# Loading the modulation rows of a two-layer recurrent backbone through GpSimd's DMA queue instead of SyncE's

## Chip, cores and metric

One Trainium2 chip, one core. The metric is the device time of one execution in microseconds. A core has five engines that run their own instruction streams in order: TensorE (PE, matmul; PEld is its weight load), VectorE (DVE), ScalarE (ACT), GpSimd (POOL) and SyncE (SP). Transfers between DRAM and on-chip memory (SBUF) are issued by an engine's instruction stream as DMAs and done by 16 DMA engines; an instruction that has to wait for a semaphore holds up all that stand behind it on its engine.

## What is computed

```python
for layer in range(2):
    mod_l = silu(c) @ w_ada[layer] + b_ada[layer]         # 6 x 1024: shift, scale, gate, twice
    mod_c = silu(c_ctx) @ w_ada[layer] + b_ada[layer]
    pl = split_proj(modulate(xl, sh1_l, sc1_l) @ w_in[layer])      # xl: 1024 latent tokens x 1024
    pc = split_proj(modulate(xc, sh1_c, sc1_c) @ w_in[layer])      # xc: 256 context tokens
    mixed = hgrn2, mlstm, retention, gla of (pc, pl)               # forward and backward chunk scans
    xl = xl + g1_l * mixer_out(raw_l, pl, g_heads[layer], w_out[layer])
    xl = xl + g2_l * (relu(modulate(xl, sh2_l, sc2_l) @ w_ff1[layer]) ** 2 @ w_ff2[layer])
    # the context xc likewise, in layer 0 alone
return rmsnorm(xl) * g_final
```

All inputs are float32. The modulation vectors `mod` depend on the conditioning `c` and `c_ctx` alone: 2 layers x 6144 values x 2 conditionings, each a dot product over 1024.

## The kernel before

All 1280 tokens stay on the chip with the 1024 features in 8 tiles of 128 partitions. Dense products are done as three matmuls each, on values split into a high and a low part (`mm3`, L292 to L296). Weights come through `whalf` (L276): SP loads 128 x 512 floats into a small ring `st` (L281), ACT makes the high part (L282), DVE the low part (L283).

A layer has four stages: a norm with the modulation applied, the mixers (`mixers`, L1422), the output projection (`outproj`, L1508) and the MLP (`mlp`, L488). In `mixers` the scans of four head groups run on DVE, ACT and PE, and the dense projections that later groups need are mixed in as filler for PE (`Fill`, L157). Projections are written to DRAM from a ring of temporaries in `st` (L689, L734, L735, L743) and fetched again (L695, L756); outputs go out at L710, gates read them at L647 and store at L658; mLSTM loads its row factors at L1326.

The first third of layer 0's modulation is a matmul at the start. Its other two thirds and the three thirds of layer 1 are computed on DVE by `ada_rows` (L402) in slack time: for a third r, a conditioning j and a half h of the 1024 inputs, the conditioning is loaded broadcast to all partitions from the scratch tensor `d_c` (L410), then 16 tiles `w_adaR` of 128 rows x 512 inputs (256 KB each, L413), and each is multiplied by it and summed along the row by one DVE instruction (L414, shown in the profile as a SCALAR_TENSOR_TENSOR and a DVE_READ_ACCUMULATOR):

```python
c = cs.next()(512)
queue.dma_start(c..., self.d_c[j:j + 1, 4 * h:4 * h + 4, :].to_broadcast([128, 4, 128]))
for o in range(16):
    w = wring.next()(512)
    queue.dma_start(w, self.io["w_adaR"][l, r, o, :, 512 * h:512 * h + 512])
    nc.vector.scalar_tensor_tensor(w, w, 1.0, c, ..., accum_out=S[:, o:o + 1, h])
```

The function is called in two places, and `queue` is SP in both. In the mixers of layer 0 (`ada`, L1597) it makes 128 row loads into two buffers of the tile `ph`, with one conditioning buffer; `Fill.step` advances it at three of five filler steps. In the MLP of layer 0 (`ada1`, L1608, advanced by `filler`) it makes 128 row loads into five buffers (two in `pc`, three in `st`), again with one conditioning buffer. A row load waits until the L414 that last read its buffer is done.

POOL itself has little to do: the store of `d_c` at the start (L333), memsets of a column of ones for the mLSTM values (L768, ten in a layer), of two slices of the mLSTM state (L1291, L1292, two pairs in a layer), and five subtractions in the norm behind the MLP (L485). The order of the instructions on each engine comes from the framework's scheduler, which sees the dependences of the whole program.

Of the kernel before, what the change touches and what calls it, by code (L numbers as in the profile page):

```python
# [42 lines left out]
class Ring:  # L43
# [4 lines left out]
    def next(self):  # L48
        x = self.items[self.i % len(self.items)]
        self.i += 1  # L50
        return x
# [1521 lines left out]
def build(ctx, tc, io):  # L1573
    b = K(ctx, tc, io)
    b.setup()
    nc = b.nc
    b.l = 0
    b.openX()
    for k in range(NK):
        nc.scalar.dma_start(b.X[k][:, 0:CTX], io["xT"][:, k, 0:CTX])  # L1580
    b.params(b.tmps.next())

    ps, ss = b.pool("ps", [512] * 16)
    bk = b.banks.next()
    ring = Ring(ss)
    for k in range(NK):
        b.ada_unit(0, 0, k, bk, ring)
    b.ada_finish(0, 0, bk, b.banks.next(), b.tmps.next())
    ps.release()
    b.params2(b.tmps.next())  # L1590
    b.cond_rows(b.tmps.next())
    for l in range(2):
        b.l = l
        tbs = TBS if l == 0 else TBS[1:]
        b.mix_open(l)

        def ada(bufs):  # L1597
            for r in (1, 2):
                yield from b.ada_rows(0, r, (0, 1), Ring(bufs[:2]), Ring(bufs[2:]), nc.sync)
        b.mixers(l, ada)  # L1600
        b.outproj(l)
        na = 3
        nf = 2 if l == 0 else 0
        nw = (b.rest - NK * NT - na * 2 * NT - 512 * nf) // 1024
        pc, cs = b.pool(f"pc{l}", [1024] * nw + [512] * nf + [NT] * (2 * na))
        wring = Ring(cs[:nw])
        aring = Ring(zip(cs[nw + nf::2], cs[nw + nf + 1::2]))
        def ada1(bufs, l=l):  # L1608
            for r in range(3) if l == 0 else ():
                yield from b.ada_rows(1, r, (0, 1) if r == 0 else (1,), Ring(bufs[:5]), Ring(bufs[5:]), nc.sync, 2)  # L1610
        tmps = b.tmps
        gen = ada1(cs[nw:nw + nf] + tmps.items[4:])

        def filler():
            for _ in range(3):
                next(gen, None)
        if l == 0:
            b.tmps = Ring(tmps.items[:4])
        first = [b.wtile(io["w_ff1"][l, f], wring) for f in range(2)]
        b.norm_block(l, tbs[-1], 24, 32, fast=FAST[5])  # L1620

        def after(tb, l=l):
            if l == 1:
                b.final_block(tb)
            elif tb[0] != TBS[-1][0]:
                b.norm_block(1, tb, 0, 8, nc.gpsimd if tb[0] else None, FAST[6] if tb[0] else FAST[7])
        b.mlp(l, tbs, wring, aring, filler, first, after)
        b.tmps = tmps
        pc.release()
    b.final_norm(*b.late)  # L1630
    b.poolX.release()
# [110 lines left out]
```

## Time and profile before

| | us |
|---|---|
| median of 3 runs | 3276.86 (3276.39 to 3285.53) |
| the profiled execution | 3277.57, span 3275.8 |
| PE busy | 3188.0 (97%) |
| DVE busy | 2098.3 (64%) |
| ACT busy | 1285.0 (39%) |
| POOL busy | 11.5 |
| bytes read and written in HBM | 259.11 and 45.65 MB, 93 GB/s over the span |

Busy time leaves out instructions that only wait or issue a DMA; for POOL the issuing instruction is counted. An average over the span says little of a single stage: the stages have different limits, and what matters is which wait ends last in each. The span divides into the start (to about 40 us), layer 0's norm and mixers (to about 780), its output projection (to about 910), its MLP (to about 1800), and layer 1 in the same order. The changed loads lie between 226 and 720 us and between 915 and 1120 us.

### The profile page before, as it was taken

To read this page: it belongs to the slowest core of one execution; us is meant where nothing else is said; L and a number is where in the kernel's file an instruction comes from. 1 tells how busy PE (TensorE), PEld (TensorE's weight loads), DVE (VectorE), ACT (ScalarE), POOL (GpSimd) and SP (SyncE) were. 2 spreads that over 40 slices of the span, in tenths; PEclk is the share of its full clock that TensorE was granted. 3 is DMA by queue.
4 is the path that set the end of the run, shared out by engine and by line. 5 is a ranking of instruction groups with operands and counts; after the bars stand their busy time and mean duration, and the time that the engine had idled before them with its cause. 6 is when DMAs were issued, how large, how long until landed. Compare 5 with 4: busy or idle time off the path is not lost.

```text
span 3275.8 us, 52563 instructions
## 1 busy us (share of the span) xinstructions
PE 3188.0 (97%) x20681; PEld 2607.3 (80%) x20681; DVE 2098.3 (64%) x4333; ACT 1285.0 (39%) x2665; POOL 11.5 (0%) x42
## 2 busy tenths in 40 slices
PE   7999999999999999999999999999999999999998
PEld 4787788878888888888888677788778888888887
DVE  4778887776588845454545586876756555555546
ACT  4666564545332121212122575764444322222222
POOL 0000000000000000000000000000000000000000
PEclk9999899999999999999999999999999999999999
DMA  6115566345157511111111212333224111111111
GB/s 208 58 61 176 183 186 190 120 134 179 63 165 230 161 39 39 39 39 39 39 39 40 78 64 73 120 109 113 90 72 151 58 46 52 46 52 46 52 49 65
DMA packets 181953, 308.20 MB, mean 94 GB/s; under 512 B 21880, under 2 KB 51240, under 8 KB 181448
## 3 DMA queue, kind: packets, MB, share of 16 engines
q1 hardware_dynamic: 180376, 303.02, 28.8%
q8 instruction: 162, 2.65, 0.3%
q10 hardware_dynamic: 1296, 1.81, 0.2%
q14 instruction: 87, 0.71, 0.1%
q0 software_dynamic: 32, 0.01, 0.0%
HBM read 259.11 MB, written 45.65 MB: 93 GB/s over the span
## 4 chain that ended last, share of the span: by engine, by line
PE 81%; DVE 8%; DMA 6%; ACT 3%; issue 1%; SPq 0%; DVEq 0%; ACTq 0%
PE psum L294 22%; PE psum L295 21%; PE psum L296 21%; PE psum L831 2%; PE psum L601 2%; PE psum L834 1%; PE psum L818 1%; PE psum L632 1%; DMA ph<-w_adaR 1%; PE psum L634 1%; PE psum L633 1%; PE psum L1359 1%; PE psum L706 1%; PE psum L1019 1%; DMA ps<-w_ada 1%
## 5 line engine op out<-in xcount | busy, mean ns | idle before, releaser
L526 DVE SCALAR_TENSOR_TENSOR x<-psum,st,x 128x512 f32<-128x512 f32 (+1 forms) x648 | 440.7, 689 | 203.5 <-PE psum L296 202.8
L282 ACT ACTIVATE pc<-st 128x512 fp32r<-128x512 f32 x256 | 161.2, 632 | 854.4 <-PE psum L295 840.9
L295 PE MATMUL psum<-pc,pc 128*128 128x512 f32 (+1 forms) x1296 | 477.0, 368 | 6.0 <-DVE pc L506 6.0
L294 PE MATMUL psum<-pc,pc 128*128 128x512 f32 (+1 forms) x1296 | 476.1, 367 | 0.0
L296 PE MATMUL psum<-pc,pc 128*128 128x512 f32 (+1 forms) x1296 | 474.7, 366 | 0.0
L294 PE MATMUL psum<-Hhi,pc 128*128 128x512 f32 (+1 forms) x1280 | 471.1, 368 | 1.5 <-ACT pc L282 1.5
L295 PE MATMUL psum<-Hlo,pc 128*128 128x512 f32 (+1 forms) x1280 | 472.0, 369 | 0.1
L296 PE MATMUL psum<-Hhi,pc 128*128 128x512 f32 (+1 forms) x1280 | 470.5, 368 | 0.0
L294 PE MATMUL psum<-Hhi,pw 128*128 128x512 f32 (+1 forms) x1192 | 451.5, 379 | 7.6 <-ACT pw L282 3.5
L295 PE MATMUL psum<-Hlo,pw 128*128 128x512 f32 (+1 forms) x1192 | 447.5, 375 | 0.0
L296 PE MATMUL psum<-Hhi,pw 128*128 128x512 f32 (+1 forms) x1192 | 446.6, 375 | 0.6 <-DVE pw L283 0.6
L505 DVE TENSOR_TENSOR st<-st 128x256 f32<-128x256 f32 (+1 forms) x160 | 101.8, 637 | 301.5 <-ACT pc L504 300.8
L295 PEld LDWEIGHTS psum<-pc,pc 128*128 128x128 f32 x1296 | 245.0, 189 | 48.4 <-DVE pc L506 6.9
L294 PEld LDWEIGHTS psum<-pc,pc 128*128 128x128 f32 x1296 | 245.0, 189 | 44.1 <-DVE x L526 1.2
L296 PEld LDWEIGHTS psum<-pc,pc 128*128 128x128 f32 x1296 | 244.6, 189 | 42.9 <-issue 2.7
L294 PEld LDWEIGHTS psum<-Hhi,pc 128*128 128x128 f32 x1280 | 241.3, 189 | 43.3 <-ACT pc L282 2.4
L295 PEld LDWEIGHTS psum<-Hlo,pc 128*128 128x128 f32 x1280 | 241.3, 189 | 41.0 <-issue 0.5
L283 DVE TENSOR_TENSOR pc<-st,pc 128x512 fp32r<-128x512 f32 x256 | 175.6, 689 | 153.4 <-ACT pc L282 133.5
L296 PEld LDWEIGHTS psum<-Hhi,pc 128*128 128x128 f32 x1280 | 241.1, 188 | 41.0 <-DVE pc L283 0.6
L294 PEld LDWEIGHTS psum<-Hhi,pw 128*128 128x128 f32 x1192 | 227.3, 191 | 53.7 <-issue 9.2
L296 PEld LDWEIGHTS psum<-Hhi,pw 128*128 128x128 f32 x1192 | 227.1, 191 | 39.3 <-issue 2.4
L295 PEld LDWEIGHTS psum<-Hlo,pw 128*128 128x128 f32 x1192 | 227.6, 191 | 37.7 <-issue 2.9
(401 smaller groups left out, 4859.4 us busy)
## 6 DMA issues: line engine op xcount, KB each, us to landing
st<-w_ff SPq DMA_DIRECT2D x256, 256.0 KB
ph<-w_adaR SPq DMA_DIRECT2D x128, 256.0 KB
st<-w_inT SPq DMA_DIRECT2D x96, 256.0 KB
st<-w_adaR SPq DMA_DIRECT2D x74, 256.0 KB
pc<-w_adaR SPq DMA_DIRECT2D x54, 256.0 KB
st<-w_out SPq DMA_DIRECT2D x50, 256.0 KB
d_z<-st SPq DMA_DIRECT2D x40, 256.0 KB
ps<-w_ada SPq DMA_DIRECT2D x32, 256.0 KB
```

Source lines behind the costliest of these rows:

```text
L282: nc.scalar.activation(hi, raw, AF.Copy)
L283: (eng or nc.vector).tensor_tensor(lo, raw, F(hi), op=ALU.subtract)
L294: t.matmul(out, lhsT=w[0], rhs=m[0], start=first, stop=False)
L295: t.matmul(out, lhsT=w[0], rhs=m[1], start=False, stop=False)
L296: t.matmul(out, lhsT=w[1], rhs=m[0], start=False, stop=last)
L505: nc.vector.tensor_tensor(r, r, r, op=ALU.mult)
L526: nc.vector.scalar_tensor_tensor(x, ps, self.mod[:, l, 40 + o, j:j + 1], x, op0=ALU.mult, op1=ALU.add)
L601: t.matmul(ps[:, 0:304], lhsT=h[a], rhs=u[b], start=(k + i == 0), stop=(k == NK - 1 and i == 2))
L632: t.matmul(ps[:, e, :], lhsT=h[0], rhs=u[0], start=(k == 0), stop=False)
L633: t.matmul(ps[:, e, :], lhsT=h[0], rhs=u[1], start=False, stop=False)
L634: t.matmul(ps[:, e, :], lhsT=h[1], rhs=u[0], start=False, stop=(k == NK - 1))
L831: nc.tensor.matmul(o, lhsT=ST[r0:r0 + kd, c, d, :], rhs=qd[d](c)[r0:r0 + kd, :], start=(j == 0), stop=False, tile_position=(r0, 0))
```

## The change

Both calls of `ada_rows` get GpSimd's queue. The 256 row loads and 16 conditioning loads are issued by POOL; every other transfer stays where it was.

```diff
         def ada(bufs):
             for r in (1, 2):
-                yield from b.ada_rows(0, r, (0, 1), Ring(bufs[:2]), Ring(bufs[2:]), nc.sync)
+                yield from b.ada_rows(0, r, (0, 1), Ring(bufs[:2]), Ring(bufs[2:]), nc.gpsimd)
...
         def ada1(bufs, l=l):
             for r in range(3) if l == 0 else ():
-                yield from b.ada_rows(1, r, (0, 1) if r == 0 else (1,), Ring(bufs[:5]), Ring(bufs[5:]), nc.sync, 2)
+                yield from b.ada_rows(1, r, (0, 1) if r == 0 else (1,), Ring(bufs[:5]), Ring(bufs[5:]), nc.gpsimd, 2)
```

The scheduler then lays out the streams anew. On SP, in the mixers of layer 0 while mLSTM runs (`d_u` its row factors, `w_inT` weight tiles, `d_z` spilled projections), before and after:

```order
-L413 DMA ph_0_256<-w_adaR 128x512
-L281 DMA st<-w_inT 128x512
-L413 DMA ph_0_256<-w_adaR 128x512
+L281 DMA st<-w_inT 128x512 x4
 L1326 DMA px_0_693<-d_u 128x384 x2
-L281 DMA st<-w_inT 128x512
 L1326 DMA ph_0_256<-d_u 128x384
-L281 DMA st<-w_inT 128x512 x2
```

The row loads are gone from SP, and the weight loads that stood among them have moved together.

On POOL, in the same mixers, from the first pair of state memsets to behind the second, in the changed program (before, the two pairs followed each other with nothing between, after ten L768):

```order
L1291 MEMSET px_0_693 128x65
L1292 MEMSET px_0_693 128x65
L413 DMA ph_0_256<-w_adaR 128x512 x8
L410 DMA ph_0_256<-d_c 128x512
L413 DMA ph_0_256<-w_adaR 128x512 x16
L410 DMA ph_0_256<-d_c 128x512
L413 DMA ph_0_256<-w_adaR 128x512 x10
L1291 MEMSET px_0_693 128x65
L1292 MEMSET px_0_693 128x65
L413 DMA ph_0_256<-w_adaR 128x512 x6
```

The second pair now stands behind 107 row loads (73 before the first pair and 34 between the two), and the ten L768 stand among the loads 38 to 61.

On DVE, in the MLP of layer 0 (`x` the residual, `pc_2` and `pc_3` weight tiles, `pc_5` a row buffer):

```order
 L526 SCALAR_TENSOR_TENSOR x_6_7732<-psum,st,x_6_7732 128x512
+L283 TENSOR_TENSOR pc_2_8587<-st,pc_2_8587 128x512
+L526 SCALAR_TENSOR_TENSOR x_7_7733<-psum,st,x_7_7733 128x512
+L283 TENSOR_TENSOR pc_3_8588<-st,pc_3_8588 128x512
 L414 SCALAR_TENSOR_TENSOR pc_5_8590,st<-pc_5_8590,st 128x512
-L526 SCALAR_TENSOR_TENSOR x_7_7733<-psum,st,x_7_7733 128x512
-L283 TENSOR_TENSOR pc_2_8587<-st,pc_2_8587 128x512
-L283 TENSOR_TENSOR pc_3_8588<-st,pc_3_8588 128x512
 L414 SCALAR_TENSOR_TENSOR st<-st 128x512 x3
```

One multiplication has moved three places back; the three that follow keep their place.

## Rows read from the trace of the kernel before

**Rows 1.** The page's first part: busy us (share of the span) and instructions of PE.

```profile
PE 3188.0 (97%) x20681; PEld 2607.3 (80%) x20681; DVE 2098.3 (64%) x4333; ACT 1285.0 (39%) x2665; POOL 11.5 (0%) x42
```

**Rows 2.** Busy time by stretch: us, then per engine (instructions), clock, DMA share, GB/s.

```profile
core 0: us, PE busy (x) PEld busy (x) DVE busy (x) ACT busy (x) POOL busy (x), PEclk, DMA share, GB/s
40.00:130.00 90.00, 87.65 (x522) 66.01 (x521) 63.31 (x139) 56.37 (x114) 0.00 (x0) 1.00 0.26 83
...
226.00:725.00 499.00, 474.51 (x4242) 381.93 (x4242) 407.88 (x1095) 276.59 (x666) 1.53 (x14) 0.97 0.52 165
910.00:1125.00 215.00, 208.12 (x1066) 177.17 (x1065) 181.30 (x440) 52.80 (x93) 0.00 (x0) 0.98 0.64 206
1125.00:1730.00 605.00, 605.00 (x3154) 520.36 (x3153) 302.99 (x483) 123.58 (x218) 0.00 (x0) 1.00 0.12 39
```

**Rows 3.** Line L414: what ended DVE's idle time before it (us, times).

```profile
  DMA st<-d_c: 19.0, 7
  DMA ph<-w_adaR: 15.5, 23
  DMA st<-w_adaR: 3.2, 8
  DMA ph<-d_c: 2.8, 3
  DMA pc<-w_adaR: 2.2, 4
```

**Rows 4.** PE's waits, 910 to 1130 us: us in total, times, longest.

```profile
PE psum L295 <- DVE pc L506: 6.0, 2, 5.4
```

**Rows 5.** SP's own waits at L413, mixers and MLP: us in total, times, longest.

```profile
SPq L413 <- DVE ph L414: 106.0, 73, 8.0
...
SPq L413 <- DVE st L414: 44.9, 58, 4.0
SPq L413 <- DVE pc L414: 43.1, 38, 4.8
```

**Rows 6.** Chain of waits: start us, us from SP's issue to the instruction released.

```profile
504.59 3.02 DMA ph<-w_adaR
...
514.75 5.01 DMA ph<-w_adaR
...
1051.34 4.37 DMA st<-d_c
```

**Rows 7.** Line L413: SP's issues in the mixers, ns min/median/max.

```profile
L413 SPq DMA_DIRECT2D ph<-w_adaR x128: 327/328/1659, 227.0 to 714.6; - x128
```

**Rows 8.** Timeline of POOL: start us, us, instruction.

```profile
24.85 0.64 POOL L333 DMA_DIRECT2D d_c<-st  x1 [24.41 <-DVE st L332]
```

**Rows 9.** DMA queues and issues, 24.5 to 30.5 us; last number: us to landing.

```profile
q1 hardware_dynamic: 1164, 2.12, 99.5%
...
d_c<-st POOLq DMA_DIRECT2D x1, 8.0 KB, 4.9
```

**Rows 10.** Timeline of SP: a small store and the load that reads it.

```profile
105.41 2.02 SPq L1226 DMA_DIRECT2D d_e<-ph  x2
107.84 1.06 SPq L1232 DMA_DIRECT2D ph<-d_e  x2
```

**Rows 11.** Waits of DVE and ACT for SP's other transfers, 226 to 725 us.

```profile
DVE px L1336 <- DMA px<-d_u: 4.1, 6, 1.1
...
ACT ph L867 <- DMA px<-d_b: 3.8, 2, 3.5
ACT pw L282 <- DMA st<-w_inT: 3.3, 1, 3.3
```

**Rows 12.** Timelines of POOL, SP and PE around the second pair of state memsets.

```profile
607.08 0.15 POOL L1291 MEMSET px<- 128x65 f32 x1 [122.71 <-DVE px L1376]
...
621.17 0.33 SPq L413 DMA_DIRECT2D ph<-w_adaR  x1
...
630.45 0.49 PE L1345 MATMUL psum<-px 64*128 64x130 f32 x4 [0.43 <-DVE px L803]
```

## The prediction

> **What bounds the kernel now.** I read the page first: TensorE (PE) is busy for 3188.0 of the 3275.8 us span [rows 1], so a change that adds no matmul can win or lose only what PE idles or falls behind. Then the table by stretch, for the two stretches in which the changed transfers run [rows 2]. In the first (226 to 725 us, layer 0's mixers) PE is busy 474.5 of 499.0 us, so it idles 24.5 us; VectorE (DVE) is busy 407.9 us and idles 91.1. In the second (910 to 1125, the first part of layer 0's MLP) PE idles 6.9 of 215 us, with DVE busy 181.3. From 1125 to 1730 PE is busy all 605 us: what is lost before is not made up there. So these two stretches hold 31.4 us of idle PE, and no gain here can exceed that by much.
>
> Then I asked who waits for the changed transfers. Only DVE does, at L414, which multiplies a row tile by the conditioning: 23 + 3 waits of 15.5 + 2.8 us in the mixers, and 7 + 8 + 4 waits of 19.0 + 3.2 + 2.2 us in the MLP [rows 3]. These are 45 waits and 42.7 us, 18.3 of them in the mixers and 24.4 in the MLP. In the MLP they have just used up what slack there was: PE waits once for 5.4 us (6.0 in two) on DVE's L506, behind those multiplications [rows 4]. Last I asked why a row comes late. SyncE (SP) was itself already waiting for an L414 that frees the buffer 73 times in the mixers and 58 + 38 times in the MLP [rows 5]. That is 169 of the 256 rows, each issued when its buffer came free. For those no queue can issue sooner; what counts is the time from issue to use.
>
> **The change, part by part.** (1) 256 row loads and 16 conditioning loads leave SP's stream and enter GpSimd's (POOL's). The bytes, the buffers (two in the mixers, five in the MLP, one conditioning tile) and the waits on L414 stay.
>
> (2) The time from issue to use. From SP it is 3.0 to 5.0 us for rows on the chain of waits, and 4.4 us for a conditioning load [rows 6]. POOL's own figure for such a load is not in the trace; its only DMA is the 8 KB store of L333. It occupies POOL for 0.64 us, where SP takes 0.33 (median) to issue a row, and it lands 4.9 us after its issue [rows 7 to 9]. The nearest SP transfer is L1226, a small store to DRAM too: issued at 105.41, and L1232, which reads it back, could be issued at 107.84, so at most 2.4 us [rows 10]. Extra delay of POOL, per load: at least 0.64 - 0.33 = 0.3 us (the issue alone; a gain below that is excluded for a row whose buffer ended the wait, since such a row cannot be issued earlier), at most 4.9 - 2.4 = 2.5 us. POOL's store ran while the DMA engines were 99.5% occupied by SP's queue, SP's in a stretch where they were 26% busy [rows 2, 9], so the top is too high. I take 1.1 us, under the middle of 1.4. The Trainium skill (DMA: Bandwidth & Descriptors, Latency and other measured facts) gives about 0.6 us to the first byte for a transfer issued from SP or ACT and about 1 us from GpSimd; by that the difference would be an estimated 0.4 us and the sum below 3283 instead of 3301 us; no run here shows either figure.
>
> (3) What that costs in the MLP. The 7 conditioning waits have one buffer, so each grows by the whole delay: 7 x 1.1 = 7.7 us. The 12 row waits share five buffers, several loads being under way at once; I count half: 12 x 1.1 / 2 = 6.6 us. Sum 14.3 us, passed on whole, since PE already waits at the end of this stretch and has no idle time behind it.
>
> (4) What it costs in the mixers. 26 waits x 1.1 = 28.6 us more of DVE standing still. DVE idles 91.1 us there, 18.3 of it for these loads, so some 73 us of idle time that waits for PE and ScalarE (ACT) could take part of it. But PE itself waits on DVE in that stretch. Between nothing and all I take half: 14.3 us.
>
> (5) What SP gains. It no longer stands at L413 (106.0 us on L414 in the mixers alone [rows 5]), so what is queued behind comes sooner. Who waits for that? The largest waits are 4.1 us (d_u), 3.8 us (d_b) and 3.3 us (a weight tile) [rows 11], 11.2 us in all. Some rows that SP now issues late, behind other transfers, also come earlier. I credit 5 us; ends 0 and 12.
>
> (6) What is queued with the loads on POOL. Ten L768 memsets and two pairs L1291/L1292 now stand between row loads that wait for DVE. The second pair comes behind the 107th row load, which SP issued at 621.17; so the memset moves from 607.08 to 622 or later. The matmul L1345 that reads it ran at 630.45 [rows 12]. I cost this at nothing: 8 us of cover; if DVE falls further behind, the excess stops PE. The five L485 subtractions on POOL come after the last of the loads.
>
> (7) The scheduler's order changes by a few places on DVE and PE. DVE's rows stay as close together as before; I cost this at nothing, with 5 us either way in the range.
>
> Sum: + 14.3 + 14.3 - 5 = + 23.6 us. In short, each microsecond of extra delay costs 26 us (28.6 / 1.1), less 5. The profiled execution took 3277.57 us (its span and 1.8 us around it), 0.7 above the median 3276.86 of three runs. 3277.6 + 23.6 = **3301.2 us**.
>
> **The rivals.** *Hardly later (0.22).* If POOL's load is later only by the longer issue, 0.3 us, the loss is 26 x 0.3 - 5 = + 3 us: 3280.6, no change that can be told. For it: of 3.0 us from issue to use SP's issue is 0.33 [rows 6, 7]; the rest is the transfer, whose bytes stay. Against it: POOL's one DMA lands after 4.9. It is also the case that the skill's two latencies above lead to.
>
> *As late as POOL's one store (0.17).* At 2.5 us the same sum gives 26 x 2.5 - 5 = + 60: 3337.6 us. For it: that row is the only one of this queue. Against it: its busy DMA engines. A cause that would hold here all the time is that POOL's preparation of a transfer is held up while DVE works, as DVE is busy 407.9 of 499.0 us in the mixers. The Trainium skill has such a rule (SBUF — State Buffer, SBUF: two separate sides, the box on DVE blocking DMA): while DVE runs an operation in a two-port mode, GpSimd can't write its descriptors. It names a plain fp32 copy for it, and DVE's work here is mostly products of two tensors; no run here shows it.
>
> *SP was the brake (0.15), the other side: faster.* If POOL's loads come no later than SP's (0.2 us or less, which is the point from which it decides: 26 x 0.2 is what SP gains), only the relief stays. The place is the mixers, the price half of the 11.2 us above, half of the 5.4 us with which PE waited in the MLP, and a third of the 18.3 us of DVE's waits, for rows that stood behind other transfers: 5.6 + 2.7 + 6.1 = 14.4: 3263.2 us. Against it: 169 rows are issued the moment their buffer is free.
>
> **How the numbers follow.** The forecast (0.7 to 1.8 us of extra delay, 3291 to 3319) has 0.46, the rivals 0.22, 0.17 and 0.15. A measurement of this kernel tells 0.3%, some 9.8 us. Faster by more: most of the last rival, 0.13. Within: the first rival, the rest of the last and the low end of the forecast, 0.29. Slower: 0.58. The range takes in the first rival and part of the last, to 3267, and goes up to a delay of 2.3 us, 3332.
>
> **What would show it.** L410 and L413 stand on POOL, with some 1 us each. DVE's waits before L414 grow from 42.7 us to between 70 and 100; PE idles more in both stretches, above all at L506 around 1120 us. SP's waits at L413 are gone, and the waits on d_u, d_b and weights shrink a little. From 1125 us on the two traces run alike, displaced. If DVE's waits at L414 do not grow, the delay is wrong and rival one or three holds; if they grow and PE's idle time does not, the half and the whole that I passed on are wrong; if PE stands at L1345 for a memset, (6) is.

## The result, and the profile after

| us | before | changed |
|---|---|---|
| median of the runs timed together | 3276.39 (5 runs, 3271.83 to 3285.53) | 3296.48 (5 runs, 3294.21 to 3298.38) |
| the profiled execution | 3277.57 | 3294.21 |
| its span | 3275.8 | 3292.4 |

The changed kernel is slower: ratio 1.0058, 95% interval 1.0045 to 1.0071, some 15 to 23 us. The forecast was 3301.2.

The page's first part, of the changed kernel, answers to [rows 1]; under it SP's and POOL's DMA queues over the whole span (packets, MB, share of 16 engines):

```profile
PE 3195.3 (97%) x20681; PEld 2613.1 (79%) x20681; DVE 2100.6 (64%) x4333; ACT 1286.0 (39%) x2665; POOL 157.3 (5%) x314
...
q1 hardware_dynamic: 141208, 231.70, 21.9%
q0 software_dynamic: 21792, 71.33, 7.0%
```

The span grew by 16.6 us. PE's idle time (span less busy) went from 87.8 to 97.1 us, so 9.3 of the 16.6 are idle PE. The other 7.3 are a PE that is longer busy with the same 20681 matmuls: the mean granted clock fell from 0.990 to 0.988. The trace's record of the clock knows two levels; at the lower, 0.50, PE spent 66.3 us of the span before and 75.9 now, and at half speed the 9.5 us more are 4.8 us of lost work.

The same stretches as in [rows 2], and then two wider ones that serve for all kernels below, since the stages shift by some us (columns as there):

```profile
226.00:725.00 499.00, 467.80 (x4178) 376.90 (x4177) 402.21 (x1078) 271.83 (x656) 73.90 (x149) 0.97 0.52 163
910.00:1125.00 215.00, 205.61 (x1042) 174.41 (x1042) 174.09 (x414) 51.90 (x91) 70.05 (x131) 0.98 0.61 195
1125.00:1730.00 605.00, 603.38 (x3140) 518.73 (x3139) 309.42 (x506) 122.88 (x216) 2.81 (x6) 1.00 0.13 42
...
226.00:735.00 509.00, 477.80 (x4240) 384.65 (x4240) 409.60 (x1096) 276.01 (x664) 74.44 (x150) 0.97 0.52 161
920.00:1180.00 260.00, 248.99 (x1276) 211.81 (x1276) 204.16 (x475) 59.30 (x104) 72.86 (x136) 0.98 0.55 177
```

Of the kernel before, the two wider ones:

```profile
226.00:735.00 509.00, 484.51 (x4286) 390.21 (x4286) 412.64 (x1104) 278.21 (x669) 1.53 (x14) 0.97 0.51 162
920.00:1180.00 260.00, 253.88 (x1312) 217.16 (x1311) 205.84 (x480) 61.32 (x108) 0.00 (x0) 0.99 0.55 176
```

In the mixers PE now idles 31.2 us where it idled 24.5, in the MLP 11.0 where it idled 6.1. That is 11.6 us more, all of the lost idle time and a little over. From the MLP's second part on PE is busy throughout, and nothing is made up.

Who waits? L414 of the changed kernel, as in [rows 3], then PE's wait of [rows 4] in the MLP:

```profile
  DMA ph<-w_adaR: 34.3, 39
  DMA st<-d_c: 18.1, 7
  DMA st<-w_adaR: 6.6, 10
  DMA pc<-w_adaR: 4.7, 10
  DMA ph<-d_c: 4.0, 3
```

```profile
PE psum L295 <- DVE pc L506: 10.1, 4, 6.7
```

DVE's waits grew from 42.7 us in 45 to 67.7 us in 69: in the mixers from 18.3 to 38.3, in the MLP from 24.4 to 29.4. Above all there are more of them: 39 waits for `ph` rows instead of 23.

Why are the rows later? POOL's issues at L413 in the mixers (ns min/median/max), against SP's 327/328/1659 in [rows 7]; the landing of all 256 row loads after the start of their issue; and the page's median of the mixers' 128:

```profile
L413 POOL DMA_DIRECT2D ph<-w_adaR x128: 536/536/574, 226.9 to 725.1; - x128
...
DMA to landing us min/median/max: 2.6/3.6/7.0
...
ph<-w_adaR POOLq DMA_DIRECT2D x128, 256.0 KB, 3.4
```

More telling is the moment at which the issue begins. First the kernel before, one release of a buffer by DVE (start us, us) and the issue that waited for it:

```profile
505.75 0.08 DVE L414 DVE_READ_ACCUMULATOR ph<-ph 128x1 f32 x1
...
505.86 0.33 SPq L413 DMA_DIRECT2D ph<-w_adaR  x1
```

The buffer is free at 505.83 and SP begins at 505.86, 0.03 us later. In the changed kernel:

```profile
508.89 0.08 DVE L414 DVE_READ_ACCUMULATOR ph<-ph 128x1 f32 x1
...
509.27 0.54 POOL L413 DMA_DIRECT2D ph<-w_adaR  x1 [0.70 <-DVE ph L414]
```

Free at 508.97, begun at 509.27: 0.30 us later. These two values are no accident of one place. Over all loads that have a multiplication ahead of them, 206 of 255 issues on SP began 0.02 to 0.06 us after the end of a multiplication, and 226 of 255 on POOL 0.28 to 0.33 after it. From its issue on a load is later too. Those for which DVE stood waiting hide it (medians from the start of the issue to use of 3.7 us before and 3.6 after), since they are not the same loads: 23 before, 39 after. The trace has the completions of each load, sixteen of them. Over all 128 loads of the mixers the last came 3.06 us after the start of the issue in the median from SP and 3.35 from POOL; the quickest took 2.39 and 2.73. Where the queue held no other transfer, the first packet moved 0.96 us after the start of the issue from SP and 1.25 from POOL (medians of 20 and 57 row loads).

So POOL's own delay is some 0.27 us before the issue starts and some 0.3 after it, for nearly every load. From the release of the buffer to the landing, both together, the medians are 3.14 us before and 3.65 after in the mixers, 3.64 and 4.18 in the MLP: half a microsecond.

SP's waits at L413 [rows 5] are gone. They are now POOL's (us, times, longest), and SP waits at other lines instead:

```profile
POOL ph L413 <- DVE ph L414: 278.9, 86, 40.1
POOL st L413 <- DVE st L414: 59.2, 41, 4.8
POOL pc L413 <- DVE pc L414: 49.1, 30, 5.3
...
SPq L281 <- DVE pw L283: 71.4, 30, 8.8
```

The consumers of [rows 11] hardly gained (226 to 725 us):

```profile
ACT ph L867 <- DMA px<-d_b: 3.7, 1, 3.7
DVE px L1336 <- DMA px<-d_u: 3.6, 7, 0.9
...
ACT pw L282 <- DMA st<-w_inT: 1.2, 1, 1.2
```

8.5 us against 11.2. And the memset of [rows 12] now stands behind a row load:

```profile
621.79 0.55 POOL L413 DMA_DIRECT2D ph<-w_adaR  x1 [4.79 <-DVE px L1353]
622.32 0.17 POOL L1291 MEMSET px<- 128x65 f32 x1
```

The L1345 matmuls ran from 600.8 to 670.6 us, and PE's only wait at that line there was 0.8 us, for a product of DVE.

### The profile page after: what moved, and what is told of

Read it like the earlier page. It is cut to its first block, busy times and chain, and to the rows that moved or that the text cites. A ratio compares the mean times of both kernels' runs of the same rounds, so it can differ in the third digit from the quotient of the medians.

```text
span 3292.4 us, 52609 instructions
## 1 busy us (share of the span) xinstructions
PE 3195.3 (97%) x20681; PEld 2613.1 (79%) x20681; DVE 2100.6 (64%) x4333; ACT 1286.0 (39%) x2665; POOL 157.3 (5%) x314
## 4 chain that ended last, share of the span: by engine, by line
PE 73%; issue 8%; DVE 8%; DMA 6%; ACT 3%; POOL 2%; SPq 0%; POOLq 0%; DVEq 0%; ACTq 0%
PE psum L294 20%; PE psum L295 20%; PE psum L296 20%; PE psum L601 2%; PE psum L831 2%; PE psum L834 1%; DMA ph<-w_adaR 1%; PE psum L818 1%; PE psum L632 1%; PE psum L634 1%; PE psum L633 1%; PE psum L448 1%; POOL ph L413 1%; DMA px<-d_u 1%; PE psum L1359 1%
## 5 line engine op out<-in xcount | busy, mean ns | idle before, releaser
L526 DVE SCALAR_TENSOR_TENSOR x<-psum,st,x 128x512 f32<-128x512 f32 (+1 forms) x648 | 440.9, 690 | 204.4 <-PE psum L296 203.9
```

Of the source, the lines that this page charges most:

```text
L526: nc.vector.scalar_tensor_tensor(x, ps, self.mod[:, l, 40 + o, j:j + 1], x, op0=ALU.mult, op1=ALU.add)
```

## The experiments

Two theories stood against each other. **A**: the queue. Each load starts later after its buffer comes free, DVE waits for it, and part of that reaches PE. **B**: the order. The scheduler lays the streams out anew, and that order is worse by itself. PE's order in the changed kernel differs from the one before in 2057 of 17329 places, all by the mixers' part: with the MLP's loads alone moved, PE's order stays as it was.

Differences below are ratio less one, times 3276 us, with the 95% interval. Beside e1 to e4 the kernel before took 3274.47 us (15 runs), beside e5 to e8 3275.70 (21), beside e9 to e12 3277.75 (15).

**Each call by itself (e1, e2).** The mixers' loads alone on POOL, then the MLP's alone:

```diff
-                yield from b.ada_rows(0, r, (0, 1), Ring(bufs[:2]), Ring(bufs[2:]), nc.sync)
+                yield from b.ada_rows(0, r, (0, 1), Ring(bufs[:2]), Ring(bufs[2:]), nc.gpsimd)
```

```diff
-                yield from b.ada_rows(1, r, (0, 1) if r == 0 else (1,), Ring(bufs[:5]), Ring(bufs[5:]), nc.sync, 2)
+                yield from b.ada_rows(1, r, (0, 1) if r == 0 else (1,), Ring(bufs[:5]), Ring(bufs[5:]), nc.gpsimd, 2)
```

> Only the mixers' loads (128 rows, 8 conditioning loads) go through GpSimd's queue, those of the MLP stay on SyncE's. Theory A (each load is usable some 0.6 us later after its buffer comes free: POOL starts it 0.30 us after the release against 0.04 and takes 0.54 us against 0.33; DVE waits for it, and half of that reaches PE): DVE's waits before L414 in the mixers 35 to 42 us as in the changed kernel, those in the MLP back at 24 us; the time 8 to 12 us above before, 3284 to 3289. Theory B (the scheduler's new order costs the time, not the queue): the mixers' order is that of the changed kernel, so about the same 8 to 12 us here; this run splits the sum between the two stretches and does not tell A from B.

> Only the MLP's loads go through GpSimd's queue. Theory A: DVE's waits before L414 in the MLP about 29 us against 24, PE's wait for L506 about 10 us against 6, the time 4 to 8 us above before, 3280 to 3285; mixers as before. Theory B: the order of the mixers and of layer 1 is the old one, so that the 3 us that the changed kernel lost in layer 1, where no such load runs, are gone as well; 3280 to 3284.

e1 took 3290.94 us, + 16 (10 to 22), a little over A's range; e2 3282.12, + 7.5 (4 to 11). Both parts lose, the mixers twice as much, and their sum of 23.6 agrees with the whole change (15 to 23) within the intervals. e2 matters for B: its PE, ACT and SP streams (without the loads) stand exactly as before, and on DVE only some 90 of the 4077 instructions in the trace (accumulator reads not counted) stand in another place. A loss without a new order on PE speaks for A.

**Three row buffers in the mixers, on POOL and on SP (e3, e4).** The edit as e3 has it, on the changed kernel; e4 is the same on the kernel before, with `nc.sync` in the last lines:

```diff
-        ao = hp.alloc(1536, True) if l == 0 else None
+        ao = hp.alloc(2048, True) if l == 0 else None
...
-            fill.also = ada([ao.sub(512 * i, 512) for i in range(3)])
+            fill.also = ada([ao.sub(512 * i, 512) for i in range(4)])
...
-                yield from b.ada_rows(0, r, (0, 1), Ring(bufs[:2]), Ring(bufs[2:]), nc.gpsimd)
+                yield from b.ada_rows(0, r, (0, 1), Ring(bufs[:3]), Ring(bufs[3:]), nc.gpsimd)
```

> The changed kernel with three row buffers in the mixers instead of two, so that a row may take one multiplication longer to come. Theory A: DVE's waits before L414 in the mixers fall from 38 us to under 15, and the 10 us that the mixers lost come back; the time 3280 to 3287. Theory B: the waits fall, but the order is again another one and the time stays at 3293 to 3300.

> The kernel before with three row buffers in the mixers, loads on SyncE's queue. Theory A: DVE's 18 us of waits before L414 in the mixers fall under 8 and PE gets back about half of the difference: 3268 to 3273. Theory B: no relation; the time moves by up to 10 us either way with the order.

e3 took 3303.44 us, + 30 (26 to 35), slower than the changed kernel: a miss of A as it was put. e4 took 3277.51, + 3 (- 2 to + 9), no difference: a miss too, since A wanted a gain. L414's waits for `ph` rows did fall, to 11.4 us in e3 and 3.9 in e4, but in e3 those for the one conditioning buffer rose from 4.0 to 15.6. Where did e3 lose? The trace in steps of 5 us, just before mLSTM's scan:

```profile
545.00:550.00 5.00, 5.00 (x41) 4.31 (x40) 1.29 (x5) 2.05 (x7) 0.73 (x2) 1.00 0.98 309
550.00:555.00 5.00, 3.35 (x29) 3.15 (x28) 1.03 (x6) 1.51 (x4) 1.07 (x2) 1.00 0.99 369
555.00:560.00 5.00, 2.95 (x25) 2.29 (x23) 3.12 (x11) 0.00 (x0) 1.61 (x3) 0.71 0.66 228
560.00:565.00 5.00, 5.00 (x41) 3.64 (x39) 1.73 (x6) 0.57 (x3) 0.00 (x0) 0.50 0.10 39
565.00:570.00 5.00, 5.00 (x43) 3.85 (x40) 1.96 (x10) 1.35 (x5) 0.00 (x0) 0.50 0.08 25
570.00:575.00 5.00, 5.00 (x32) 4.52 (x31) 4.87 (x18) 1.67 (x6) 0.00 (x0) 0.59 0.35 93
```

The chain of waits of e3 over the same stretch (start us, us):

```profile
543.71 5.58 DMA ph<-w_adaR
549.32 0.71 DVE ph L414 x2
550.05 0.19 DVE st L418
550.31 5.40 DMA ph<-d_c
```

A row and then the conditioning took over 5 us each while the DMA engines were 98 to 99% busy; PE stood 3.7 us out of ten, and then its granted clock fell to 0.50, the lower of its two levels (1.2 of 2.4 GHz), for some 17 us (a mean of 0.71 and of 0.59 in a stretch of 5 us is 2.9 and 4.1 us at the lower level, with the 10 between). At half speed these 17 us do the work of 8.5, so the clock cost over twice what the wait itself did. In the changed kernel DVE waited 3.3 us in the same place, PE stood 1.4 us and the clock stayed at 1.00:

```profile
570.00:575.00 5.00, 3.58 (x38) 2.94 (x36) 4.02 (x13) 2.47 (x9) 1.07 (x2) 1.00 0.96 337
```

This is a third cost, which neither theory had. It is not all of e3's loss: over the whole of the mixers (226 to 735 us) PE spent 37.5 us at the lower level in e3, and 34.1 in the changed kernel at other places. Nor does the length of a stand alone tell when the clock falls. The kernel before has a stretch as long, from 335.4 to 352.5 us, and PE had stood only 1.6 us in the ten before it (a further 5.0 us during it):

```profile
330.00:360.00 30.00, 23.37 (x163) 17.53 (x162) 22.53 (x52) 15.61 (x30) 0.00 (x0) 0.72 0.42 134
```

**The MLP: buffers and delay (e5, e6, e7).** In the MLP a second conditioning buffer in place of the fifth row buffer, on POOL (e5, shown) and on SP (e6, the same with `nc.sync`, on the kernel before), then the changed kernel with a delay added in POOL's stream (e7; `several` is 2 in the MLP alone):

```diff
-                yield from b.ada_rows(1, r, (0, 1) if r == 0 else (1,), Ring(bufs[:5]), Ring(bufs[5:]), nc.gpsimd, 2)
+                yield from b.ada_rows(1, r, (0, 1) if r == 0 else (1,), Ring(bufs[:4]), Ring(bufs[4:]), nc.gpsimd, 2)
```

```diff
-                queue.dma_start(c.rearrange("p (k q) -> p k q", q=128), self.d_c[j:j + 1, 4 * h:4 * h + 4, :].to_broadcast([128, 4, 128]))
+                several < 2 or nc.gpsimd.memset(c, 0.0); queue.dma_start(c.rearrange("p (k q) -> p k q", q=128), self.d_c[j:j + 1, 4 * h:4 * h + 4, :].to_broadcast([128, 4, 128]))
...
-                    queue.dma_start(w, self.io["w_adaR"][l, r, o, :, 512 * h:512 * h + 512])
+                    several < 2 or nc.gpsimd.memset(w, 0.0); queue.dma_start(w, self.io["w_adaR"][l, r, o, :, 512 * h:512 * h + 512])
```

> The changed kernel with two conditioning buffers and four row buffers in the MLP (instead of one and five). The order of PE, ACT and SP stays that of the changed kernel (six places of PE's 17329 rows differ); of DVE's rows some 200 of 4063 stand elsewhere. Theory A (each load is usable some 0.6 us later after its buffer is free, and DVE waits for it): L414's 7 waits for st<-d_c (18.1 us) go, the row waits grow by a few us since a buffer is taken from them, PE's 10.1 us at L506 shrink below 3; the time comes 6 to 10 us below the changed kernel, 10 to 14 above the one before. Theory B (the new order of the streams costs the time, not the queue): no gain, still some 20 us above the kernel before.

> The kernel before (SP's queue for all) with two conditioning buffers and four row buffers in the MLP; order of PE and ACT as in the kernel before but for six places. Theory A: L414's 19.0 us for st<-d_c go, and with them most of the 6.0 us that PE waits at L506: 3 to 6 us faster than before. If the row waits take their place (four buffers instead of five), or if PE's wait was not behind them: no difference. Theory B: no difference.

> The changed kernel, and in the MLP POOL also clears each buffer (128x512) before it issues the load into it: a delay added between the release of the buffer and the load, of the clearing's own time (to be read, 0.15 us for 65 columns, so between 0.2 and 1.2 us). PE's, ACT's and SP's order is exactly that of the changed kernel. Theory A, with the prediction's rule for the MLP (7 conditioning waits whole, 12 row waits by half, so 13 us for each us of delay): 3 to 15 us slower than the changed kernel, all of it between 920 and 1140 us, and the MLP's own loss per us of delay gives back what POOL's queue itself adds. Theory B: no difference from the changed kernel.

e5 took 3295.64 us, + 21 (17 to 25), as the changed kernel and a miss of A, which wanted 6 to 10 us less; e6 3275.72, + 2 (- 1 to + 5), as the one before. The waits for the conditioning are gone in both, and it helps nothing. Of e6, L414's waits:

```profile
  DMA ph<-w_adaR: 14.0, 21
  DMA pc<-w_adaR: 11.8, 12
  DMA st<-w_adaR: 5.2, 9
```

19.0 us of conditioning waits went, the row waits grew from 5.4 to 17.0, and PE's idle time from 920 to 1180 us stayed at 6.4 (before: 6.1). What DVE gained did not lie ahead of a product for which PE waits.

e7 took 3293.10 us, + 18 (12 to 23): no more than the changed kernel, though a clearing took 0.54 us ahead of every load. DVE's waits in the MLP rose to 39.4 us, but PE idled 11.0 as in the changed kernel. The scheduler knew the time of the clearings and put the multiplications later in DVE's order: the last of them is the 2114th instruction of DVE in e7's trace, in the changed kernel the 2091st. The rows of the last loads, e7 and then the changed kernel:

```profile
L413 POOL MEMSET pc<- x54: 524/544/553, 932.0 to 1155.2; 128x512 f32 x54
L413 POOL DMA_DIRECT2D pc<-w_adaR x54: 536/536/547, 932.9 to 1156.0; - x54
```

```profile
L413 POOL DMA_DIRECT2D pc<-w_adaR x54: 536/536/545, 926.2 to 1131.5; - x54
```

A delay that the scheduler sees is partly covered by its order. A fails here as a rule of so many us for each us of delay.

**The conditioning loads alone, the row loads alone (e8, e11).** Both on the kernel before; e8 issues the 16 loads of L410 by POOL, e11 the mixers' 128 of L413:

```diff
-                queue.dma_start(c.rearrange("p (k q) -> p k q", q=128), self.d_c[j:j + 1, 4 * h:4 * h + 4, :].to_broadcast([128, 4, 128]))
+                nc.gpsimd.dma_start(c.rearrange("p (k q) -> p k q", q=128), self.d_c[j:j + 1, 4 * h:4 * h + 4, :].to_broadcast([128, 4, 128]))
```

```diff
-                queue.dma_start(c.rearrange("p (k q) -> p k q", q=128), self.d_c[j:j + 1, 4 * h:4 * h + 4, :].to_broadcast([128, 4, 128]))
+                (nc.sync).dma_start(c.rearrange("p (k q) -> p k q", q=128), self.d_c[j:j + 1, 4 * h:4 * h + 4, :].to_broadcast([128, 4, 128]))
...
-                yield from b.ada_rows(0, r, (0, 1), Ring(bufs[:2]), Ring(bufs[2:]), nc.sync)
+                yield from b.ada_rows(0, r, (0, 1), Ring(bufs[:2]), Ring(bufs[2:]), nc.gpsimd)
```

> The kernel before with only the 16 conditioning loads (8 in the mixers, 8 in the MLP) issued by POOL; the 256 row loads stay on SP. In the mixers the order changes as much as by the whole change (2083 of PE's 17329 places differ from the kernel before, against 2057). Theory A: the mixers lose 2 us or less (3 waits on the conditioning), the MLP 3 to 5 us (7 waits by 0.6 us): 3 to 7 us slower than before. Theory B: a new order in the mixers costs about what it cost in the changed kernel, 8 us and more at the end of the mixers.

> The kernel before with the 128 row loads of the mixers on POOL; the conditioning loads, and all of the MLP's, stay on SP. PE's order differs from the kernel before in 1282 of 17329 places. Theory A: the rows carry the loss of the mixers; L414's waits for ph<-w_adaR are 28 to 36 us as in the changed kernel, PE's idle time between 226 and 735 us is some 6 us more than before (31 against 25), and the time 10 to 16 us above the one before. Theory B (a new order alone): 2 to 6 us above, as with the conditioning loads alone.

e8 took 3280.67 us, + 6 (2 to 10); its output projection began 2.7 us later than before, where B wanted 8 and more, with as many places of PE's order changed as by the whole change. e11 took 3298.52, + 22 (15 to 29): the row loads alone carry all of the mixers' loss, and more than expected. L414 of e11:

```profile
  DMA ph<-w_adaR: 46.4, 40
```

**Two conditioning buffers in the mixers, and a delay in the mixers (e9, e10).** Both on the changed kernel; e9 has e3's allocation of 2048 with `Ring(bufs[:2])` kept, so that two buffers are left for the conditioning; e10:

```diff
-                    queue.dma_start(w, self.io["w_adaR"][l, r, o, :, 512 * h:512 * h + 512])
+                    several > 1 or nc.gpsimd.memset(w, 0.0); queue.dma_start(w, self.io["w_adaR"][l, r, o, :, 512 * h:512 * h + 512])
```

> The changed kernel with two conditioning buffers beside the two row buffers in the mixers of layer 0 (the MLP unchanged). Here a theory that came out of the run with three row buffers: there the single conditioning buffer let DVE stand 4.4 us at once, PE idled and its granted clock fell to half for some 16 us. If that wait was what made that run slow, then with two conditioning buffers the L414 waits for ph<-d_c go (4.0 us), the row waits stay near 34 us, and the time is 0 to 5 us below the changed kernel: 15 to 20 above the one before. Theory B (any new order costs): anything between 10 and 30 above the one before, without relation to the waits.

> The changed kernel; in the mixers POOL also clears each row buffer (128x512, 0.54 us) before it issues the load into it, so each row comes some 0.54 us later still. Theory A with the prediction's rule for the mixers (39 row waits, half of the delay reaches PE): L414's waits for ph<-w_adaR grow from 34 to some 50 us, and the time by 0.54 x 39 / 2 = 10 us over the changed kernel, some 30 above the one before. If the scheduler, which knows the clearing's time, moves the multiplications back as it did in the MLP (no loss there): 0 to 4 us over the changed kernel. Theory B: no relation to the delay.

e9 took 3302.07 us, + 27 (22 to 32): a miss. The waits for `ph<-d_c` fell to 1.8 us, but in e3's place a row load was now late. Chain of waits, and steps of 5 us, of e9:

```profile
555.34 7.51 DMA ph<-w_adaR
```

```profile
560.00:565.00 5.00, 4.06 (x34) 3.85 (x33) 1.80 (x5) 1.06 (x3) 1.07 (x2) 1.00 0.82 305
565.00:570.00 5.00, 2.42 (x14) 1.89 (x16) 2.55 (x8) 0.38 (x1) 1.07 (x2) 0.85 0.80 263
570.00:575.00 5.00, 5.00 (x39) 3.56 (x39) 1.87 (x6) 0.57 (x3) 0.00 (x0) 0.50 0.05 20
575.00:580.00 5.00, 5.00 (x44) 3.93 (x45) 1.91 (x9) 1.12 (x4) 0.00 (x0) 0.50 0.02 5
580.00:585.00 5.00, 5.00 (x30) 4.57 (x30) 3.60 (x16) 0.58 (x3) 0.00 (x0) 0.50 0.45 116
```

Again PE stood 3.5 us and ran at half clock for some 17 us. So it was not the conditioning buffer alone that made e3 slow. In all of e9's mixers PE spent 54.6 us at the lower level, 20.5 more than in the changed kernel, which is 10 us of lost work. The two runs have the place in common: where mLSTM begins, SP's transfers (two loads of `d_v`, 650 KB each, among them) hold the DMA engines while DVE waits for a load from POOL. With three buffers on SP (e4) the clock there stayed at 1.00. Why DVE's wait there is 3.3 us in the changed kernel, 5.5 in e9 and 3.6 and 4.4 one after the other in e3 was not told apart.

e10 took 3308.53 us, + 32 (26 to 37), some 13 more than the changed kernel, where the rule for the mixers gave 10. But the waits for rows grew by 6 us only (40.5), not by 16; PE's idle time in the mixers grew by 7.3, to 38.5. The sum was about right, the path to it only in part.

**The MLP's loads on ScalarE (e12).**

```diff
-                yield from b.ada_rows(1, r, (0, 1) if r == 0 else (1,), Ring(bufs[:5]), Ring(bufs[5:]), nc.sync, 2)
+                yield from b.ada_rows(1, r, (0, 1) if r == 0 else (1,), Ring(bufs[:5]), Ring(bufs[5:]), nc.scalar, 2)
```

> The kernel before with the MLP's 136 loads issued by ScalarE instead of SP (the mixers stay on SP). PE's order differs from the kernel before in 39 places. If what the MLP lost is POOL's own delay: PE idles some 6 us between 920 and 1185 us as before (not 11), L414's waits stay near 24 us, and the time is within 3 us of the kernel before. If it came from leaving SP as such (loads that now compete with SP's weight tiles instead of standing in one line with them): 5 to 7 us slower, as on POOL. If ScalarE, which waits in order at each load, is held up: slower still, with PE waiting for ACT at L282 and at the relu.

3281.36 us, + 4 (0 to 8), between the theories' values. ACT begins an issue 0.03 us after the release, as SP does, but its own work then stands behind the loads:

```profile
ACT st L503 <- DMA st<-w_adaR: 24.3, 5, 5.7
```

PE idled 9.5 us in the MLP. This run does not separate POOL's delay from leaving SP.

**All kernels side by side.** PE's idle time is the length of the stretch less PE's busy time in it (226 to 735 and 920 to 1180 us); DVE's waits in the mixers are L414's two `ph` rows together.

```
                    mixers: queue  DVE's waits  PE idle   MLP: queue   PE idle   time
before                      SP        18.3        24.5         SP         6.1      0
e6                          SP        16.4        22.6         SP         6.4     +2
e4 (3 row buffers)          SP         6.5        21.4         SP         7.8     +3
e12                         SP        17.6        23.0         ACT        9.5     +4
e8 (conditioning on POOL)   SP        18.7        25.9         SP         9.4     +6
e2                          SP        17.6        23.5         POOL      12.0     +7.5
e1                          POOL      37.6        31.0         SP         7.0    +16
e11 (rows on POOL)          POOL      48.5        38.4         SP         7.6    +22
e7                          POOL      37.9        31.0         POOL      11.0    +18
changed                     POOL      38.3        31.2         POOL      11.0    +19
e5                          POOL      38.9        30.6         POOL      10.2    +21
e9                          POOL      42.4        32.2         POOL      10.9    +27
e3 (3 row buffers)          POOL      27.0        35.7         POOL      11.1    +30
e10                         POOL      42.5        38.5         POOL      10.3    +32
```

Read by the queue columns. In the mixers PE idles 21.4 to 25.9 us in the six kernels with row loads on SP, and 30.6 to 38.5 in the eight with them on POOL, in five different orders of PE's work among the latter alone. In the MLP it is 6.1 to 7.8 us with all loads on SP, 10.2 to 12.0 with them on POOL. The orders scatter within each group; the queue separates the groups. e8 and e12, with a part of the MLP's loads on POOL or all of them on ACT, lie between. The clock goes with the mixers' queue as well: over the whole span PE spent 54.6 to 69.7 us at the lower level in the six kernels, 75.9 to 93.5 in the eight. B alone falls. None of the twelve is faster than the kernel before.

The columns of waits and idle time come from one execution each, the time from the medians: e7's profiled execution took 3301.07 us and e10's 3302.29, so these two rows do not show what parts their medians.

## Why the prediction was right, and where not

The sign, the range and the place were right: DVE's waits at L414 grew to 67.7 us, a little under the 70 to 100 that were named, PE idles more in both stretches, and the SP waits at L413 are gone. POOL's issues took 0.54 us, not some 1. That the sum (+ 23.6) came near the measured 19 is luck: errors in its terms cancelled.

- **(2), the delay per load, is the term that was mis-sized most.** Taken: 1.1 us, with 0.7 to 1.8 for the forecast; shown: half a microsecond from the release of the buffer to the landing. The 0.3 us after the start of the issue are the lower end that was argued. The 0.27 us between release and issue were not in the sum, which let both queues begin at the same moment. The first rival, *Hardly later*, had only the 0.3. The Trainium skill's two latencies (DMA: Bandwidth & Descriptors, Latency and other measured facts) gave an estimated 0.4 us for the difference to the first byte; here the first packet moved 0.29 us later from POOL (1.25 against 0.96 us from the start of the issue).
- ***As late as POOL's one store*** had nothing for it: the median load landed after 3.35 us, not 4.9, and POOL's issues held at 0.54 us (at most 0.57 in the mixers) while DVE was busy for 402 of 499 us, so nothing shows a preparation that DVE holds up.
- **The count of 26 was as wrong, the other way.** The sum let only those waits grow that were there. But with two buffers in turn nearly every load is issued when its buffer comes free, so nearly every one is late: 128 x 0.5 = 64 us in the mixers. Of these DVE's waits show 20 (38.3 less 18.3), in 16 new waits and in longer ones. With 0.5 us and the 26 waits the sum would have been + 8, with the first rival's 0.3 its + 3; both are too little for the same reason.
- **(4), the mixers**: taken + 28.6 us of waits, half of it to PE, 14.3. Shown: + 20.0 and + 6.7 of idle PE, a third. The part alone (e1) took + 16, which lies near 14.3 because a longer busy PE came on top: 7.9 us in e1's profiled execution.
- **(3), the MLP**: taken + 14.3, half of it for the seven conditioning waits. They did not grow (19.0 to 18.1), and without them nothing is gained (e5, e6). The row waits grew by 5.9, where 6.6 were taken. PE idles 4.9 us more: DVE's additional 5.0 passed on whole, as argued, but only in these two kernels (e6's DVE waits fell by 7.4 without gain, e7's grew by a further 10.0 without loss).
- **(5), SP's relief**: credited 5. The waits of [rows 11] shrank by 2.7 us, and nothing shows a gain of PE from it. The rival *SP was the brake* has nothing for it: its condition, 0.2 us of delay or less, was not met.
- **(6), memsets**: right. The second pair moved to 622.32, as said, and PE did not wait for it.
- **(7), the order**: nothing, with 5 us either way, was about right; e8, with an order of its own, began the output projection 2.7 us later.
- **Missing: the clock.** The sum had only idle time, but a wait that lets PE idle can cost its clock for a while after, as e3 and e9 show at one place. The profiled execution of the changed kernel lost 4.8 us more to the lower level than that of the kernel before. Of these 3.1 fall behind the last L526 of layer 0, where no such load runs: PE spent 31.5 us there at the lower level against 25.4 before, and that stretch took 3.0 us longer. In the other kernels it took from 5.1 us less to 4.6 more than in the kernel before, so a stage of one execution is not to be trusted to better than some 5 us.

Open: how much of DVE's new waits the half microsecond per load explains. That the queue costs the time is shown, that it does so by this delay is argued: a further 0.6 us ahead of each issue in the mixers (e10) gave 4 us more of DVE's waits there, and a clearing ahead of each in the MLP (e7) cost nothing. Open too is why the MLP loses with loads on POOL, and already with the conditioning alone (e8), and whether SP's weight tiles now compete with these loads; e12 was meant to tell, and could not.

## What to carry to other kernels

Where a load waits for a buffer that its consumer has just freed, what a queue adds between that release and the landing comes to every load of the ring, not only to those for which the consumer is seen waiting now. Count the loads for the most that it can cost, and expect a part of it: here 64 us in the mixers, of which 20 became waits of DVE and 7 idle time of PE. Moving 272 such loads to a queue that delivers them half a microsecond later cost this kernel, which is bound by TensorE, more than the freed queue gave back, and nobody had been seen waiting long for that queue's other transfers. And price an idle TensorE with the clock that it may lose afterwards.

## What was not expected of the hardware

- POOL began a waiting DMA 0.30 us after the multiplication that freed its buffer, in 226 of 255 cases; SP (206 of 255) and ACT (e12, 96 of 128) 0.03 us. Issuing one 128 x 512 load held POOL for 0.54 us, SP and ACT for 0.33.
- From the start of its issue such a load had landed after 3.35 us from POOL and 3.06 from SP (medians of 128 in the mixers). With the DMA engines up to 99% busy by SP's traffic beside them, loads from POOL took 5.4, 5.6 and 7.5 us to their use; from SP the slowest in the mixers landed after 5.1 us in the kernel before and 6.6 in e8.
- PE ran at 0.50 of its clock for some 17 us on end, after standing 3.7 us (e3) and 3.5 us (e9) of ten, but in the kernel before also after 1.6; after 1.4 us of standing in the changed kernel it stayed at 1.00.
